# One decoder step on Trainium2: three slabs for the modulation weights, SSM-table stores on another queue, a bias broadcast in four later pieces, state copies after the attention

## The chip, the cores and the metric

The kernel runs on one core of a Trainium2 chip. The metric is the device time of one execution in microseconds (us). Engines are called as in the profile: PE (TensorE, PEld its weight loads), DVE (VectorE), ACT (ScalarE), POOL (GpSimd), SP (SyncE, which here does nothing but issue transfers). A "q" behind an engine's name is its sequencer, the part that waits on semaphores and issues transfers.

## What is computed

One layer of a hybrid decoder for a prompt of 1024 tokens and 8 sample rows, all in float32. The part that matters here, cut from the reference:

```
def adaln(c, w, b):
    m = (jax.nn.silu(c) @ w + b)[:, None, :]          # 9 rows x 6144 columns
    return jnp.split(m, 6, axis=-1)
def shared_bias(table, dist):
    bt = table[rel_bucket(dist)]                       # 8 heads
    return jnp.moveaxis(bt, -1, 0).reshape(N_KV_HEADS, GQA, *dist.shape)
```

Around it stand a state-space model (SSM, "S5") on half of the mixer's channels, attention with that bias on the other half (compressed, selected and window keys), and a top-4-of-32 mixture of experts. One of the outputs, win_kv_sample, is the sample rows' window state of 512 tokens moved on by one token.

## The kernel before

The program is one stream of stages; a scheduler turns the order in which the instructions are written into a fixed order on each engine.

1. **Before the mixer, 0 to 403 us.** Five jobs are written in turns, as the string ORDER (line 35) says: `adaln` (24 turns "r"), `compress_sample` (the sample rows' cache), the statistics of x, `ssm_prep` (turn "S") and `bias_prep` (turn "B"). Then `mixer_x` normalizes x.
   - `adaln` loads w_ada in 24 slabs `wt` of 128x8x256 (1 MB each, on SP, L499) into two buffers; each slab feeds 8 matmuls (L504), and the next load into a buffer waits for these.
   - `compress_sample` transposes gathered cache rows `rr` on PE (L1155), splits them into `xh` (ACT, L1157) and `xl` (DVE, L1158) and multiplies them (L475 to L477).
   - `ssm_prep` computes, in 8 iterations over groups g0, the tables of the SSM: six products on POOL (`lmul`, L885), transposes on PE into `o1` (L922), a product with `v1` (L937), copies on ACT (L924 to L926, L938), sums on DVE. Each iteration stores `o1` (L927), `v1` (L933), `wt` (L947) to `ssmw` and zeros (`zt`, L940) and `kt` (L941) to `ssmk`, all on SP. The name `tp` is a PSUM buffer, `wt` here another tile than adaln's.
   - `bias_prep` stores a row of 1152 biases for each of 8 heads (`bt`, L1249) and copies each 128 times, from DRAM to DRAM, to `bx` (L1251, 4.7 MB), which the attention reads back (`tt`, L1305) with a skewed pattern.
2. **Mixer, 403 to 685 us** (`mixer`, L633). Seven blocks of 256 columns, a = 0, 256, ..., 1536. In each, for the 8 row tiles t, 24 matmuls (L475 to L477) fill a PSUM bank. For a < 512 ACT copies it to a tile `kv` (L689; two buffers) and SP stores it to `ud` (L690). From a = 256 to a < 1280 one of the 16 steps of `ssm` is written at each odd t: a step loads `w` (L976) and `m` (L980) of the tables and `hs` (L1023, L1024), every fourth step also `ur` from `ud` (L970), then transposes (`up`, L986) and goes through DVE and ACT; at its end it stores `hb` (L1052).
3. **Attention, 685 to 1200 us.** It reads `bx`, stores its result (`attd`, L1389, on SP); the sample rows' part copies 511 rows of window state from DRAM to DRAM for each of 8 sample rows (L1700, 0.5 MB each, on SP). The scheduler has put these copies into stage 1.
4. **Mixture of experts, 1200 to 3207 us**: weight streams and matmuls with an order of their own.

On each queue the transfers are issued in order. A transfer counts on one of eight semaphores of its queue, taken in turn.

Of the kernel before, what the change touches and what calls it, by code (L numbers as in the profile page):

```python
# [10 lines left out]
F = mybir.dt.float32  # L11
# [11 lines left out]
D = 1024  # L23
B = 8
NT = T // 128
KT = D // 128
# [424 lines left out]
class K:  # L451
# [28 lines left out]
    def adaln(self, c):  # L480
        nc, tc, i = self.nc, self.tc, self.i
        self.md = tc.dram_tile([9, 6144], F, name="md")
        p = self.pool("ada", ctx=c)
        w = self.pool("adaw", bufs=2, ctx=c)
        q = self.pool("adaq", bufs=1, psum=True, ctx=c)
        cs, sg = (w.tile([128, KT, 256], F, name="wt").rearrange("p k f -> p (k f)")[:9, :D] for _ in range(2))
        nc.sync.dma_start(out=cs[0:8], in_=i["c_sample"])
# [8 lines left out]
        for n in range(24):  # L496
            s = slice(n * 256, (n + 1) * 256)
            wt = w.tile([128, KT, 256], F, name="wt")
            nc.sync.dma_start(out=wt, in_=i["w_ada"][0].rearrange("(k p) f -> p k f", p=128)[:, :, s])  # L499
            bt = w.tile([9, 256], F, name="bt")  # L500
            nc.scalar.dma_start(out=bt, in_=i["b_ada"][:, s].to_broadcast([9, 256]))
            po = q.tile([128, 256], F, name="po")[:9]
            for k in range(KT):
                last = nc.tensor.matmul(po, lhsT=ct[:, k], rhs=wt[:, k], start=k == 0, stop=k == KT - 1)  # L504
            self.ada.append(last.ins)
            mt = w.tile([9, 256], F, name="mt")
            one = 1.0 if n // 4 in (1, 4) else 0.0
            nc.vector.scalar_tensor_tensor(out=mt, in0=po, scalar=one, in1=bt, op0=ALU.add, op1=ALU.add)
            nc.scalar.dma_start(out=self.md[:, s], in_=mt)
            yield  # L510
# [53 lines left out]
    def mixer_x(self):  # L564
        nc, i = self.nc, self.i
        p, q, hp, mv, rs = self.csp, self.csq, self.hp, self.mv, self.rs
# [3 lines left out]
        rows = p.tile([16, 128], F, name="fold", bufs=2)  # L570
# [5 lines left out]
        for t in range(NT):  # L576
# [16 lines left out]
            (nc.vector if t in ON_DVE2 else nc.gpsimd).tensor_tensor(out=self.hl[:, :, s], in0=h32, in1=self.hh[:, :, s].bitcast(F), op=ALU.subtract)  # L593
        xq, sh, sc = (p.tile([8, D], F, name="rr", bufs=4) for _ in range(3))
        nc.sync.dma_start(out=xq, in_=i["x_sample"][:, 0])
# [37 lines left out]
    def mixer(self, ctx):  # L633
# [9 lines left out]
        with ExitStack() as c:  # L643
# [4 lines left out]
            for m, (a, n) in enumerate(((0, 256), (256, 256), (512, 256), (768, 256), (1024, 256), (1280, 256), (1536, 280))):  # L648
# [31 lines left out]
                for t in range(NT):  # L680
# [6 lines left out]
                    if a < 512:  # L687
                        ut = p2.tile([128, 256], F, name="kv")
                        nc.scalar.activation(out=ut, in_=po[:, :256], func=AF.Copy)  # L689
                        nc.sync.dma_start(out=self.ud.rearrange("m t f -> (m t) f")[rows, a:a + 256], in_=ut)  # L690
                    elif a < 1024:
# [77 lines left out]
    def ssm_prep(self):  # L769
# [11 lines left out]
        with ExitStack() as c:  # L781
# [128 lines left out]
            zt = p.tile([16, 4, 128], F, name="zt")  # L910
            g_.memset(zt, 0.0)
            p2 = self.pool("sp2", bufs=2, ctx=c)
            for g0 in range(0, 32, 4):
# [12 lines left out]
                nc.scalar.activation(out=o1[:, 1, :, 64:128], in_=tp[:, :, 0:64], func=AF.Copy, scale=-1.0)  # L926
                nc.sync.dma_start(out=self.wd_[:, 0:2, gs], in_=o1)  # L927
                v1 = p2.tile([128, 4, 9, 16], F, name="v1")
# [3 lines left out]
                v.tensor_tensor(out=v1, in0=v1, in1=w2, op=ALU.add)  # L932
                nc.sync.dma_start(out=self.wd_[:, 2, gs], in_=v1[:, :, 1:9].rearrange("p g k c -> p g (k c)"))  # L933
                kt = p2.tile([16, 4, 8, 16], F, name="kt")
# [4 lines left out]
                v.tensor_tensor(out=kt[:, :, 0], in0=kt[:, :, 0], in1=dd[:, gs], op=ALU.add)  # L939
                nc.sync.dma_start(out=self.kd[:, gs, 0:8].rearrange("c g k d -> c g (k d)"), in_=zt)  # L940
                nc.sync.dma_start(out=self.kd[:, gs, 8:16].rearrange("c g k d -> c g (k d)"), in_=kt.rearrange("c g k d -> c g (k d)"))  # L941
                wt = p2.tile([128, 4, 8, 16], F, name="wt")
# [3 lines left out]
                v.tensor_tensor(out=wt, in0=wt, in1=w2[:, :, 0:8], op=ALU.subtract)  # L946
                nc.sync.dma_start(out=self.wd_[:, 3, gs], in_=wt.rearrange("p g k c -> p g (k c)"))  # L947

# [169 lines left out]
    def compress_sample(self):  # L1118
# [16 lines left out]
        for b in range(B):  # L1135
            rr = []
# [6 lines left out]
            for ch in range(4):  # L1143
                after = self.ada[-1:][:1] if 4 * b + ch >= 8 else []
                with self.tc.issue_after(after[0]) if after else ExitStack():
# [3 lines left out]
                    for s in range(2):  # L1149
                        r = p.tile([128, 16, 64], F, name="rr", bufs=4)  # L1150
                        nc.vector.tensor_copy(out=r, in_=rr[s][:, ch])
# [63 lines left out]
    def bias_prep(self):  # L1215
# [6 lines left out]
        with ExitStack() as c:  # L1222
# [26 lines left out]
            nc.sync.dma_start(out=self.bt, in_=bv)  # L1249

            nc.sync.dma_start(out=self.bx, in_=self.bt[:, None].to_broadcast([8, 128, 1152]))  # L1251

# [25 lines left out]
    def attention(self):  # L1278
# [3 lines left out]
        with ExitStack() as c:  # L1282
# [78 lines left out]
            def values(g, t, pr):  # L1361
# [26 lines left out]
                v.tensor_tensor(out=at[hi], in0=ov[hi, :, 1], in1=sh[hi], op=ALU.add)  # L1388
                nc.sync.dma_start(out=self.att[:, 2 * g:2 * g + 2, rows], in_=at)  # L1389

# [212 lines left out]
    def sample_attention(self, bank):  # L1603
# [75 lines left out]
        with ExitStack() as c:  # L1679
# [14 lines left out]
            for b in range(B):  # L1694
# [4 lines left out]
                flat = [d[0, b].rearrange("t c h d -> (t c h d)") for d in (self.o["win_s"], i["state_win_kv"])]  # L1699
                nc.sync.dma_start(out=flat[0][0:511 * 256].rearrange("(a f) -> a f", a=128), in_=flat[1][256:512 * 256].rearrange("(a f) -> a f", a=128))  # L1700
                tp = bank(128, 4, 128)
# [618 lines left out]
```

## Time and profile before

| | |
|---|---|
| runs shown | median 3202.93 us of 3 (3199.05 to 3207.68) |
| profiled execution | 3209.21 us, span 3207.4 us, mean granted clock 0.946 |
| busy share of the span | PE 93%, DVE 72%, ACT 56%, POOL 11% |
| stage 1, 0 to 403 us | PE busy 313.1 us (68.34, 63.46, 162.52 and 18.80 in four stretches) |
| mixer, 403 to 685 us | PE busy 280.4 us |
| attention and on, 685 to 1200 us | PE busy 473.5 us |
| experts, 1200 to 3207 us | PE busy 1905.0 us |

A row of a table by stretches gives the stretch and its length, the busy time of PE, PEld, DVE, ACT and POOL with their instructions, the granted clock of PE (1.00 is the full 2.4 GHz, 0.50 is 1.2 GHz), the busy share of the core's 16 DMA engines, and GB/s. A row of a list of waits gives the waiting engine and line, what it waited for, the sum in us, how often, and the longest. In a timeline a row is start, duration, engine, line, operation, and in brackets the idle time before it and what ended it.

### The profile page before, as it was taken

To read this page: it belongs to the slowest core of one execution; us is meant where nothing else is said; L and a number is where in the kernel's file an instruction comes from. 1 tells how busy PE (TensorE), PEld (TensorE's weight loads), DVE (VectorE), ACT (ScalarE), POOL (GpSimd) and SP (SyncE) were. 2 spreads that over 40 slices of the span, in tenths; PEclk is the share of its full clock that TensorE was granted. 3 is DMA by queue.
4 is the path that set the end of the run, shared out by engine and by line. 5 is a ranking of instruction groups with operands and counts; after the bars stand their busy time and mean duration, and the time that the engine had idled before them with its cause. 6 is when DMAs were issued, how large, how long until landed. Compare 5 with 4: busy or idle time off the path is not lost. (4 is left out here: it accounts for less than half of the span.)

```text
span 3207.4 us, 51067 instructions
## 1 busy us (share of the span) xinstructions
PE 2972.0 (93%) x15681; PEld 2380.6 (74%) x15682; DVE 2321.0 (72%) x4434; ACT 1785.9 (56%) x2824; POOL 358.7 (11%) x467
## 2 busy tenths in 40 slices
PE   7787899998999898599999999999999999999977
PEld 4555699976778586378887887888887888878752
DVE  5654846448777688688878868775689865796978
ACT  3332635456657643377667656564477654675751
POOL 1620121002311000100000000000000000000013
PEclk9888899988879799699999999999999999999988
DMA  8766343223512342798979869764289915792926
GB/s 287 250 219 226 126 124 106 85 74 83 132 29 65 126 152 80 264 335 288 315 228 369 277 230 360 233 238 139 77 281 371 337 68 190 242 368 100 350 84 275
DMA packets 445575, 656.33 MB, mean 205 GB/s; under 512 B 45455, under 2 KB 371072, under 8 KB 441265
## 3 DMA queue, kind: packets, MB, share of 16 engines
q1 hardware_dynamic: 418290, 535.40, 49.7%
q0 software_dynamic: 24464, 115.59, 10.4%
q10 hardware_dynamic: 2704, 3.85, 0.3%
q8 instruction: 64, 1.05, 0.1%
q14 instruction: 53, 0.43, 0.0%
HBM read 594.95 MB, written 68.73 MB: 207 GB/s over the span
## 5 line engine op out<-in xcount | busy, mean ns | idle before, releaser
L272 DVE TENSOR_TENSOR lo<-raw,hi 128x1024 fp32r<-128x1024 f32 x870 | 1030.9, 1221 | 307.3 <-ACT hi L199 302.3
L199 ACT ACTIVATE hi<-raw 128x1024 fp32r<-128x1024 f32 x870 | 916.3, 1060 | 491.9 <-PE pc L388 490.7
L386 PE MATMUL pc<-hi,X 128*128 128x512 f32 x1408 | 561.0, 398 | 4.7 <-DVE X L277 3.8
L388 PE MATMUL pc<-hi,X 128*128 128x512 f32 x1408 | 550.8, 391 | 0.0
L387 PE MATMUL pc<-lo,X 128*128 128x512 f32 x1408 | 549.8, 390 | 0.0
L386 PEld LDWEIGHTS pc<-hi,X 128*128 128x128 f32 x1408 | 265.2, 188 | 60.6 <-issue 8.9
L388 PEld LDWEIGHTS pc<-hi,X 128*128 128x128 f32 x1408 | 264.9, 188 | 56.6
L387 PEld LDWEIGHTS pc<-lo,X 128*128 128x128 f32 x1408 | 265.5, 189 | 51.5
L386 PE MATMUL pc<-hi,HT 128*128 128x512 f32 x704 | 282.6, 401 | 12.1 <-DVE HT L294 9.0
L388 PE MATMUL pc<-hi,HT 128*128 128x512 f32 x704 | 274.8, 390 | 0.0
L387 PE MATMUL pc<-lo,HT 128*128 128x512 f32 x704 | 274.6, 390 | 0.0
L386 PEld LDWEIGHTS pc<-hi,HT 128*128 128x128 f32 x704 | 132.2, 188 | 53.4 <-issue 28.5
L388 PEld LDWEIGHTS pc<-hi,HT 128*128 128x128 f32 x704 | 132.2, 188 | 28.3
L1319 DVE CUSTOM_DVE_ANT_0 pt<-sc,tt 128x512 f32<-128x512 f32 (+7 forms) x256 | 107.3, 436 | 61.5 <-PE sc L1335 29.1
L387 PEld LDWEIGHTS pc<-lo,HT 128*128 128x128 f32 x704 | 132.4, 188 | 24.9
L475 PE MATMUL po<-wih,hh 128*128 128x256 f32 (+3 forms) x504 | 147.6, 293 | 0.0
L476 PE MATMUL po<-wil,hh 128*128 128x256 f32 (+3 forms) x504 | 146.9, 292 | 0.0
L477 PE MATMUL po<-wih,hl 128*128 128x256 f32 (+3 forms) x504 | 145.8, 289 | 0.0
L504 PE MATMUL po<-wt,ct 128*9 128x256 f32 x384 | 102.6, 408 | 38.6 <-DMA wt<-in_w_ada_dram 36.9
L421 POOL DMA_INDIRECT xg<-hd,ic x52 | 65.4, 1257 | 589.2 <-PE px L354 558.2
L1157 ACT ACTIVATE xh<-tp 128x512 fp32r<-128x512 f32 x128 | 71.3, 594 | 89.1 <-PE tp L1155 80.6
L1372 PE MATMUL tp<-ident,pt 128*128 128x128 f32 (+6 forms) x592 | 115.3, 306 | 4.4 <-DVE pt L1358 4.0
(698 smaller groups left out, 5742.6 us busy)
## 6 DMA issues: line engine op xcount, KB each, us to landing
raw<-in_w_gate_up_dram SPq DMA_DIRECT2D x248, 1024.0 KB, 10.0
raw<-in_w_down_dram SPq DMA_DIRECT2D x64, 2048.0 KB
wt<-in_w_ada_dram SPq DMA_DIRECT2D x24, 1024.0 KB
yd<-yt SPq DMA_DIRECT2D x44, 512.0 KB
w<-ssmw SPq DMA_DIRECT2D x16, 512.0 KB
raw<-in_w_gate_up_dram POOLq DMA_DIRECT2D x8, 1024.0 KB
wir<-in_w_in_dram SPq DMA_DIRECT2D x20, 256.0 KB
bx<-bt SPq DMA_DIRECT2D x1, 4608.0 KB
```

Of the source, the lines that this page charges most:

```text
L199: A.activation(out=hi[:,u%H],in_=rawview(u),func=AF.Copy).then_inc(S['hi'][u],1)
L272: V.tensor_tensor(out=lo[:,u%H],in0=rawview(u),in1=hi[:,u%H].bitcast(F),op=ALU.subtract).then_inc(S['lo'][u],1)
L386: PE.matmul(o,lhsT=sH,rhs=wh,start=kt==0,stop=False)
L387: PE.matmul(o,lhsT=sH,rhs=wl,start=False,stop=False)
L388: ins=PE.matmul(o,lhsT=sL,rhs=wh,start=False,stop=kt==7)
L475: pe.matmul(o, lhsT=lh, rhs=rh, start=start, stop=False)
L476: pe.matmul(o, lhsT=lh, rhs=rl, start=False, stop=False)
L477: return pe.matmul(o, lhsT=ll, rhs=rh, start=False, stop=stop)
L504: last = nc.tensor.matmul(po, lhsT=ct[:, k], rhs=wt[:, k], start=k == 0, stop=k == KT - 1)
L1157: nc.scalar.activation(out=xo, in_=tp, func=AF.Copy)
L1319: v.tensor_tensor_reduce(out=pt[:, off[r] + a:off[r] + a + n], in0=sc, in1=bias, scale=1.0, scalar=-3e38, op0=ALU.add, op1=ALU.max, accum_ ...
L1372: pe.transpose(tp[:n, h * 128:h * 128 + 128], pr[h][:, a:a + n], self.ident)
```

## The change

- `adaln`: three buffers for the slabs `wt` in place of two; the buffers `rr` of `compress_sample` and `mixer_x` go from four to three.
- `ssm_prep`: all stores are issued on ACT; the eight stores of zeros stand ahead of the 8 iterations.
- `bx`: the one broadcast of L1251 becomes four of two heads each (1.18 MB), on SP, each right behind the store to `ud` of t = 1, 3, 5, 7 in the mixer's block a = 256.
- the 8 copies of the window state are held behind the last attention store written before them.

```
-        cs, sg = (w.tile([128, KT, 256], F, name="wt")...
+        cs, sg = (w.tile([128, KT, 256], F, name="wt", bufs=3)...
...
-            wt = w.tile([128, KT, 256], F, name="wt")
+            wt = w.tile([128, KT, 256], F, name="wt", bufs=3)
...
-                        r = p.tile([128, 16, 64], F, name="rr", bufs=4)
+                        r = p.tile([128, 16, 64], F, name="rr", bufs=3)
...
-                        nc.sync.dma_start(out=self.ud...[rows, a:a + 256], in_=ut)
+                        st = nc.sync.dma_start(out=self.ud...[rows, a:a + 256], in_=ut)
+                        if a == 256 and t % 2:
+                            hs = slice(t - 1, t + 1)
+                            with self.tc.issue_after(st.ins):
+                                nc.sync.dma_start(out=self.bx[hs], in_=self.bt[hs, None].to_broadcast([2, 128, 1152]))
...
+            for g0 in range(0, 32, 4):
+                nc.scalar.dma_start(out=self.kd[:, g0:g0 + 4, 0:8]..., in_=zt)
...
-                nc.sync.dma_start(out=self.wd_[:, 0:2, gs], in_=o1)
+                nc.scalar.dma_start(out=self.wd_[:, 0:2, gs], in_=o1)
...
-                nc.sync.dma_start(out=self.kd[:, gs, 0:8]..., in_=zt)
...
-            nc.sync.dma_start(out=self.bx, in_=self.bt[:, None].to_broadcast([8, 128, 1152]))
...
-                nc.sync.dma_start(out=self.att[:, 2 * g:2 * g + 2, rows], in_=at)
+                self.put = nc.sync.dma_start(out=self.att[:, 2 * g:2 * g + 2, rows], in_=at).ins
...
-                nc.sync.dma_start(out=flat[0]..., in_=flat[1]...)
+                with self.tc.issue_after(self.put):
+                    nc.sync.dma_start(out=flat[0]..., in_=flat[1]...)
```

The stores of `v1`, `kt` and `wt` change in the same way as that of `o1`. In the changed kernel L922 is L929, L937 is L944, L924 to L926 are L931 to L933, the stores L927, L933, L941, L947 are L934, L940, L947, L953, L976 is L982, L980 is L986, L986 is L992, L1155 is L1161; the pieces of `bx` are L695.

The scheduler gives the engines another order. Three places follow.

**PE, the last iterations of `ssm_prep`.** Before, the transposes L922 and the products L937 of an iteration stand among slabs of `adaln` (L504) and transposes of `compress_sample` (L1155):

```order
L922 MATMUL tp<-ident,wt 128x128 x4
L937 MATMUL tp<-v_1110,bst 16x128 x4
L504 MATMUL po<-wt,ct 9x256 x8
L1155 MATMUL tp<-ident,rr 128x128 x7
L922 MATMUL tp<-ident,wt 128x128 x4
L1155 MATMUL tp<-ident,rr 128x128
L937 MATMUL tp<-v_1147,bst 16x128 x4
L1155 MATMUL tp<-ident,rr 128x128 x8
L504 MATMUL po<-wt,ct 9x256 x3
L922 MATMUL tp<-ident,wt 128x128 x4
```

After the change:

```order
L1161 MATMUL tp<-ident,rr 128x128 x7
L929 MATMUL tp<-ident,wt 128x128 x4
L944 MATMUL tp<-v_1151,bst 16x128 x4
L929 MATMUL tp<-ident,wt 128x128 x4
L944 MATMUL tp<-v_1187,bst 16x128 x4
L929 MATMUL tp<-ident,wt 128x128 x4
L944 MATMUL tp<-v_1223,bst 16x128 x4
L929 MATMUL tp<-ident,wt 128x128 x4
L944 MATMUL tp<-v_1259,bst 16x128 x4
L1161 MATMUL tp<-ident,rr 128x128 x4
```

The last four iterations follow each other with nothing between. Between the first transpose L922 and the last product L937 of all eight, the order before has 133 matmuls of L475 to L477, 84 transposes L1155 and 30 matmuls L504; the order after has 24, 22 and 16. The rest stands ahead: 72, 42 and 15 more than before precede the first transpose.

**ACT, two iterations of `ssm_prep` after the change.** Before, ACT held only the four copies here, among those of `compress_sample`, and the stores stood on SP between the loads L499:

```order
L931 ACTIVATE o_1110<-tp 128x512
L932 ACTIVATE o_1110<-tp 128x4x64
L933 ACTIVATE o_1110<-tp 128x4x64
L940 DMA ssmw<-v_1115 128x4x128
L934 DMA ssmw<-o_1110 128x2x512
L945 ACTIVATE kt<-tp 16x512
L953 DMA ssmw<-wt 128x512
L947 DMA ssmk<-kt 16x4x128
L931 ACTIVATE o_1146<-tp 128x512
```

The four stores of an iteration now stand between its copies and those of the next one.

**SP, the block a = 256 of the mixer.** After the change (the stores to `ud` here are those of t = 1 to 5; before, the same kinds of rows stand here without the broadcasts, with the loads of `w` and `m` further ahead):

```order
L690 DMA ud<-kv 128x256
L695 DMA bx<-bt 256x1x1152
L690 DMA ud<-kv 128x256
L1058 DMA out_dram<-hb 8x2x64 x2
L690 DMA ud<-kv 128x256
L695 DMA bx<-bt 256x1x1152
L690 DMA ud<-kv 128x256
L986 DMA m<-ssmk 128x1x128
L1029 DMA hs<-in_state_ssm_re_dram 8x2x64
L1030 DMA hs<-in_state_ssm_im_dram 8x2x64
L690 DMA ud<-kv 128x256
L695 DMA bx<-bt 256x1x1152
```

The stores to `ud` and a load of `m` are queued behind pieces of the broadcast. On PE, the second half of that step now stands behind 49 projection matmuls, and the whole block a = 512 (8 times 24 matmuls) stands before the products of step 3; between the end of step 3 and the `up` transposes of step 4 (L992) there is none of these, where the order before has 53.

## Rows read from the trace of the kernel before

**Rows 1.** Busy time of each engine over the span, from the page.

```profile
PE 2972.0 (93%) x15681; PEld 2380.6 (74%) x15682; DVE 2321.0 (72%) x4434; ACT 1785.9 (56%) x2824; POOL 358.7 (11%) x467
```

**Rows 2.** Table by stretches, the time before the mixer.

```profile
0.00:93.00 93.00, 68.34 (x406) 49.05 (x407) 57.34 (x168) 31.58 (x54) 15.49 (x24) 0.98 0.84 274
93.00:178.00 85.00, 63.46 (x374) 43.74 (x374) 57.46 (x75) 29.20 (x62) 58.69 (x49) 0.84 0.66 236
178.00:373.00 195.00, 162.52 (x1055) 113.96 (x1054) 109.20 (x215) 68.10 (x129) 10.87 (x19) 0.91 0.59 217
```

**Rows 3.** Waits of PE, 0 to 403 us.

```profile
PE po L504 <- DMA wt<-in_w_ada_dram: 36.9, 4, 16.5
```

**Rows 4.** Waits of SP's queue, 0 to 403 us.

```profile
SPq L499 <- PE po L504: 112.7, 16, 14.2
SPq L927 <- ACT o L926: 38.0, 6, 13.0
```

**Rows 5.** Timeline of PE at these waits, and of SP ahead of the longest.

```profile
144.18 2.30 PE L504 MATMUL po<-wt,ct 128*9 128x256 f32 x5 [7.03 <-DMA wt<-in_w_ada_dram]
...
198.90 5.58 PE L504 MATMUL po<-wt,ct 128*9 128x256 f32 x16 [9.55 <-DMA wt<-in_w_ada_dram]
204.41 0.77 PE L1155 MATMUL tp<-ident,rr 128*128 128x128 f32 x5
...
257.93 0.77 SPq L1251 DMA_DIRECT2D bx<-bt  x1
265.73 24.87 SPq L499 DMA_DIRECT2D wt<-in_w_ada_dram  x2
...
280.22 0.28 PE L476 MATMUL po<-xl,w1h 128*128 128x256 f32 x1
280.34 0.28 PE L477 MATMUL po<-xh,w1l 128*128 128x256 f32 x1
297.07 2.30 PE L504 MATMUL po<-wt,ct 128*9 128x256 f32 x5 [16.45 <-DMA wt<-in_w_ada_dram]
```

**Rows 6.** Table by stretches, while the broadcast moves, and around the wait.

```profile
261.00:270.00 9.00, 8.81 (x56) 5.77 (x56) 4.75 (x9) 3.24 (x8) 0.10 (x1) 1.00 0.51 209
...
290.00:297.00 7.00, 0.00 (x0) 0.00 (x0) 0.00 (x0) 0.00 (x0) 0.00 (x0) 0.50 0.89 307
297.00:322.00 25.00, 24.21 (x137) 14.55 (x138) 9.55 (x17) 6.48 (x13) 0.10 (x1) 0.90 0.36 123
```

**Rows 7.** Timeline of POOL, the same product of three iterations in a row.

```profile
88.07 1.06 POOL L885 TENSOR_TENSOR wt<-pw,bst 128x512 f32<-128x512 f32 x1
...
96.75 1.50 POOL L885 TENSOR_TENSOR wt<-pw,bst 128x512 f32<-128x512 f32 x1
...
106.61 1.06 POOL L885 TENSOR_TENSOR wt<-pw,bst 128x512 f32<-128x512 f32 x1
```

**Rows 8.** Groups of PE, the slabs' matmuls over the span, from the page.

```profile
L504 PE MATMUL po<-wt,ct 128*9 128x256 f32 x384 | 102.6, 408 | 38.6 <-DMA wt<-in_w_ada_dram 36.9
```

**Rows 9.** Table by stretches, the mixer's blocks with SSM steps, and the attention.

```profile
436.00:548.00 112.00, 112.00 (x1016) 106.15 (x1015) 65.68 (x223) 55.70 (x125) 18.02 (x50) 1.00 0.39 115
...
685.00:1200.00 515.00, 473.46 (x2717) 377.08 (x2718) 379.03 (x1391) 318.87 (x751) 66.17 (x87) 0.86 0.33 96
```

**Rows 10.** Timeline of SP, block a = 256 of the mixer.

```profile
445.05 0.36 SPq L690 DMA_DIRECT2D ud<-kv  x1
...
447.01 0.34 SPq L690 DMA_DIRECT2D ud<-kv  x1
...
457.07 0.35 SPq L690 DMA_DIRECT2D ud<-kv  x1
```

**Rows 11.** Transposes `up` (L986), two a step: ns, first and last start.

```profile
L986 PE MATMUL up<-ident,ug x32: 271/272/273, 436.0 to 603.3; 128*128 128x128 f32 x32
```

**Rows 12.** The copies to `kv` (L689): what ACT waited for before them.

```profile
  DMA ud<-kv: 2.7, 1
```

**Rows 13.** The copies of the window state, from the list of transfers.

```profile
out_dram<-in_state_win_kv_dram SPq DMA_DIRECT2D x8, 511.0 KB
```

More of the change, by code (lines that the diff above doesn't have):

```diff
@@ L485, in adaln @@
         q = self.pool("adaq", bufs=1, psum=True, ctx=c)
-        cs, sg = (w.tile([128, KT, 256], F, name="wt").rearrange("p k f -> p (k f)")[:9, :D] for _ in range(2))
+        cs, sg = (w.tile([128, KT, 256], F, name="wt", bufs=3).rearrange("p k f -> p (k f)")[:9, :D] for _ in range(2))
         nc.sync.dma_start(out=cs[0:8], in_=i["c_sample"])
@@ L593, in mixer_x @@
             (nc.vector if t in ON_DVE2 else nc.gpsimd).tensor_tensor(out=self.hl[:, :, s], in0=h32, in1=self.hh[:, :, s].bitcast(F), op=ALU.subtract)
-        xq, sh, sc = (p.tile([8, D], F, name="rr", bufs=4) for _ in range(3))
+        xq, sh, sc = (p.tile([8, D], F, name="rr", bufs=3) for _ in range(3))
         nc.sync.dma_start(out=xq, in_=i["x_sample"][:, 0])
@@ L689, in mixer @@
                         nc.scalar.activation(out=ut, in_=po[:, :256], func=AF.Copy)
-                        nc.sync.dma_start(out=self.ud.rearrange("m t f -> (m t) f")[rows, a:a + 256], in_=ut)
+                        st = nc.sync.dma_start(out=self.ud.rearrange("m t f -> (m t) f")[rows, a:a + 256], in_=ut)
+                        if a == 256 and t % 2:
+                            hs = slice(t - 1, t + 1)
+                            with self.tc.issue_after(st.ins):
+                                nc.sync.dma_start(out=self.bx[hs], in_=self.bt[hs, None].to_broadcast([2, 128, 1152]))
                     elif a < 1024:
@@ L911, in ssm_prep @@
             g_.memset(zt, 0.0)
+            for g0 in range(0, 32, 4):
+                nc.scalar.dma_start(out=self.kd[:, g0:g0 + 4, 0:8].rearrange("c g k d -> c g (k d)"), in_=zt)
             p2 = self.pool("sp2", bufs=2, ctx=c)
@@ L932, in ssm_prep @@
                 v.tensor_tensor(out=v1, in0=v1, in1=w2, op=ALU.add)
-                nc.sync.dma_start(out=self.wd_[:, 2, gs], in_=v1[:, :, 1:9].rearrange("p g k c -> p g (k c)"))
+                nc.scalar.dma_start(out=self.wd_[:, 2, gs], in_=v1[:, :, 1:9].rearrange("p g k c -> p g (k c)"))
                 kt = p2.tile([16, 4, 8, 16], F, name="kt")
@@ L939, in ssm_prep @@
                 v.tensor_tensor(out=kt[:, :, 0], in0=kt[:, :, 0], in1=dd[:, gs], op=ALU.add)
-                nc.sync.dma_start(out=self.kd[:, gs, 0:8].rearrange("c g k d -> c g (k d)"), in_=zt)
-                nc.sync.dma_start(out=self.kd[:, gs, 8:16].rearrange("c g k d -> c g (k d)"), in_=kt.rearrange("c g k d -> c g (k d)"))
+                nc.scalar.dma_start(out=self.kd[:, gs, 8:16].rearrange("c g k d -> c g (k d)"), in_=kt.rearrange("c g k d -> c g (k d)"))
                 wt = p2.tile([128, 4, 8, 16], F, name="wt")
@@ L946, in ssm_prep @@
                 v.tensor_tensor(out=wt, in0=wt, in1=w2[:, :, 0:8], op=ALU.subtract)
-                nc.sync.dma_start(out=self.wd_[:, 3, gs], in_=wt.rearrange("p g k c -> p g (k c)"))
+                nc.scalar.dma_start(out=self.wd_[:, 3, gs], in_=wt.rearrange("p g k c -> p g (k c)"))
     def ssm(self, c):
@@ L1699, in sample_attention @@
                 flat = [d[0, b].rearrange("t c h d -> (t c h d)") for d in (self.o["win_s"], i["state_win_kv"])]
-                nc.sync.dma_start(out=flat[0][0:511 * 256].rearrange("(a f) -> a f", a=128), in_=flat[1][256:512 * 256].rearrange("(a f) -> a f", a=128))
+                with self.tc.issue_after(self.put):
+                    nc.sync.dma_start(out=flat[0][0:511 * 256].rearrange("(a f) -> a f", a=128), in_=flat[1][256:512 * 256].rearrange("(a f) -> a f", a=128))
                 tp = bank(128, 4, 128)
```

## The prediction

> **What bounds the kernel now.** I read the page first: PE is busy 93% of the span [rows 1], so a change counts by the PE idle time that it removes or adds, or by PE's clock. The table by stretches shows where idle time is left ahead of the mixer: 93.0 - 68.3 = 24.7 us, 85.0 - 63.5 = 21.5 us and 195.0 - 162.5 = 32.5 us in three stretches, 78.7 us together [rows 2]. The list of PE's waits there names the largest: 36.9 us in four waits for slabs of `adaln` [rows 3]. They are 7.03, 9.55 and 16.45 us in the timeline [rows 5], and the fourth is what is left, 3.9 us, in the first stretch. The list for SP's queue tells why slabs are late: a slab waits for its buffer (112.7 us), and SP stands still behind SSM stores whose data are not ready, 38.0 us for those of `o1` alone [rows 4]. The longest PE wait has another neighbour: after the broadcast of `bx` at 257.93, the next two slab issues take SP 24.87 us, and PE gets its slab at 297.07 [rows 5]. In the mixer's SSM blocks there is nothing to win: PE is busy 112.0 of 112.0 us at granted clock 1.00 [rows 9]. Any stall put there is paid in full. In the attention PE has 515.0 - 473.5 = 41.5 us of idle time and the DMA engines a share of 0.33 [rows 9].
>
> **The change ahead of the mixer.** The third slab buffer, the stores taken off SP, the broadcast and the state copies taken out of the stage all work at those four waits. I let them go: -3.9 us in the first stretch, -7.0 in the second, -9.6 and -16.5 (26.0 together) in the third. What is late next is `ssm_prep`. Its eight iterations now stand close together on PE, and each needs six products on POOL. POOL is busy 58.7 us in the second stretch [rows 2], 58.7 / 8 = 7.3 us an iteration if nothing holds it; the starts of one product lie 8.7 and 9.9 us apart [rows 7]. In the order after, POOL's gathers mostly stand elsewhere, but each iteration also waits on ACT, where four stores stand between its copies and the next one's (an issue on SP is 0.35 us [rows 10]). I take 8.1 us, between the two, 65 us for eight.
>
> PE's work in those 65 us: the 63.5 us of the second stretch, less what moved out. A matmul of `compress_sample` starts 0.12 us after the one before it and a transpose takes 0.77 / 5 = 0.15 us [rows 5]; a matmul of a slab is 102.6 / 192 = 0.53 us (the 384 records are two for each of 24 x 8) [rows 8]. Moved out are 133 - 24 = 109, 84 - 22 = 62 and 30 - 16 = 14 of these: 13.1 + 9.3 + 7.4 = 29.8 us. So 33.7 us stay, and PE idles 65 - 34 = 31 us there, where it idled 21.5. The idle time ahead of the mixer becomes 20.8 + 31 + 6.5 = 58.3 in place of 78.7, -20.4 us. Behind the longest wait the granted clock was 0.50 and then 0.90 on average over 25 us [rows 6]; without it these 25 us give back some 2. **This term: -22 us.** Bounds: at 7.3 us an iteration the idle time there is 25, so -29, and with some of the other waits of the stage -35. At 9.3 us (the mean of the two distances) it is 41, so -12, and if half of the 26 us stays as waits for slabs, +1. `rr` with three buffers in place of four costs nothing while slabs or POOL set the pace; without that cover it is within these bounds.
>
> **The broadcast in the mixer.** The old transfer has eight heads in its outermost dimension; while it moves, the DMA share is 0.51, about 8 of 16 engines, at 209 GB/s [rows 6], so one engine seems to carry one head: 4.72 MB / 209 GB/s = 22.6 us. A piece has two heads. Its bytes on each of two engines are those of the old transfer, so a piece lasts 22.6 us too, four one behind the other 90 us. A store to `ud` or a load of `m` uses all engines, and its shares on the two busy ones are queued behind the piece. The trace shows no such piece, so the ends are: each on engines of its own (all four overlap), or all on the same two. I take the same two, because the one transfer that is shown had a fixed set and nothing in the second differs but its address; this decides most of the forecast.
>
> The Trainium skill, "DMA: Bandwidth & Descriptors", section "Why a DMA increments its semaphore by 16 and not by 1", says that the engines used are the largest number up to 16 that divides the outermost dimension on both sides, and the lowest-numbered ones. The trace agrees on the number (0.51 for eight heads [rows 6]); which engines, no run here shows yet. By it the pieces share two engines and the sum is the one below; by the other end it is about 40 us less.
>
> On the clock of before: the store of t = 1 is issued at 445.05 [rows 10], piece 1 right behind it and done at 468. The store of t = 2 (447.01) lands then. `kv` has two buffers, so the copy of t = 4, which came just ahead of the store at 457.07 [rows 10], waits until 468. That this wait exists the rows on that copy show, 2.7 us once [rows 12]. PE goes on with t = 5 and then lacks a bank, about 464 to 468: **5 us**. The store of t = 4 goes out at 469 behind piece 2, which ends at 491. The copy of t = 6 waits for it, and so does a load of `m` that step 2 needs. PE has t = 6 and t = 7 left, some 49 matmuls of 0.12 us, until about 474: **18 us** of idle time. Step 2 ends with little beside it: **4 us**. Then the block a = 512, 8 x 24 matmuls and its transposes, covers piece 3 (to 514). Step 3 stands alone on PE behind it. A step came every 167.3 / 15 = 11.2 us [rows 11], of which 48 projection matmuls took 48 x 0.12 = 5.8, so without them some 6 us of its chain show; and step 4's loads are queued behind piece 4, until 537, which I price at as much again: **12 us**. Steps 4 to 9 stand close together with 85 projection matmuls where there were 48 to a step, with DVE ahead of PE: **5 us**. **This term: +44 us.** Bounds: overlapping pieces end by 469 and 492, and by that the second stall is about 3 us and the third and fourth mostly gone, +10; if every us of the four pieces were paid, +90.
>
> **The rest.** The state copies move 8 x 0.5 MB [rows 13] in a stage whose DMA share is 0.33 [rows 9]; at 300 GB/s (the rate at share 0.89 is 307 [rows 6]) that is 14 us of all engines over some 500. I take +1, for loads that stand behind them, between -3 and +6. The experts' 2007 us are not touched.
>
> **Sum.** -22 + 44 + 1 = +23 us on the profiled execution's 3209 us, 3232. That execution is 6.3 us over the median of the runs shown, 3202.9; on that basis the time is **3226 us**.
>
> **The rivals.**
> A. **The pieces cost little, faster.** If the four transfers overlap, or their shares spread over many engines, the mixer loses 10 us or less and the sum is -22 + 10 + 1 = -11, **3192 us**; with nothing lost 3182. For: PE had the copies' wait only once before [rows 12], and the DMA share in the block is 0.39 [rows 9]. Against: a share of 0.51 for eight heads [rows 6], which says few engines for few heads. The mechanism decides at the store of t = 4: if it lands before 474 in the clock above, the kernel is faster. The point is a loss of 12 us in the mixer.
> B. **They cancel.** A gain of 33 us ahead of the mixer (7.3 us an iteration, clock kept) and a loss of 33 (the copies' stalls, but steps 3 to 9 hidden): **3203 us**. For: POOL's pace of 7.3 [rows 2]. Against: ACT's queue now has the stores.
> C. **The bunched iterations eat the gain.** With 9.3 us an iteration and slabs still late, the first term is about 0: +45, **3248 us**. For: distances of 8.7 and 9.9 us [rows 7].
> D. **The waits for slabs stay.** If the slabs are late because of the DMA engines (share 0.84 in the first stretch [rows 2]) and not of buffers and SP's queue, the change does not do what it says; a part of C's price.
>
> **How the numbers follow.** About 0.3%, 9.6 us, is what a measurement of this kernel can tell from no change. The forecast, which spans 3210 to 3242 by its own bounds, 0.47; A 0.22; B 0.19; C and D 0.12. Faster takes A and little else: 0.22; the same (3193 to 3213) B and the low edge of the forecast: 0.21; slower 0.57. The range leaves out A's lowest tenth and all four pieces in full: 3188 to 3258.
>
> **What would show it.** Ahead of the mixer: the four waits L504 gone but for a few us, the mixer's first matmul some 22 us earlier, PE idle some 30 us between the first L929 and the last L944. In the mixer: copies to `kv` that wait for `ud`, stretches with the DMA share near 2/16 = 0.13, and PE idle some 40 us between 410 and 530. If the share there is far above 0.13 or PE stays busy, the second term is wrong, and A holds; if waits for slabs stay above 15 us, the first.

## The result, and the profile after

The change makes the kernel slower: 3289.1 us, median of 4 runs (3280.3 to 3292.6), against 3204.3 us of the kernel before in the same runs; the ratio is 1.0256, 95% interval 1.0233 to 1.0279. The forecast was 3226 with a range up to 3258: the sign was right, the loss is 85 us in place of 23.

Both profiles can be cut at the same events: the first matmul behind the loads of phi_w (L1092, now L1098), the first transpose of `mixer_x` (L584), the first load of `tt`, the last attention store, the experts' first gather (L421). The cuts are starts read from the timelines.

| us | before | after | difference | forecast |
|---|---|---|---|---|
| start to first matmul | 13.1 | 26.1 | +13.0 | 0 |
| first matmul to `mixer_x` | 360.1 | 355.5 | -4.6 | -22 |
| `mixer_x` and mixer | 310.8 | 366.0 | +55.2 | +44 |
| attention | 412.1 | 417.6 | +5.5 | +1 |
| to the experts' first gather | 227.6 | 227.1 | -0.5 | 0 |
| experts | 1883.7 | 1895.2 | +11.5 | 0 |
| span | 3207.4 | 3287.4 | +80.0 | +23 |

The lists of PE's waits of the changed kernel, ahead of the mixer (to 382 us), and then in it (382 to 748):

```profile
PE po L1098 <- DMA fold<-in_phi_pe_dram: 21.9, 1, 21.9
PE tp L929 <- DVE wt L926: 18.5, 5, 6.4
PE po L476 <- DVE xl L1164: 14.8, 3, 12.8
PE tp L1161 <- DVE xl L1164: 14.8, 4, 7.3
```

```profile
PE po L475 <- ACT kv L689: 24.5, 2, 14.4
PE up L992 <- DVE ug L989: 9.6, 1, 9.6
```

The 36.9 us of waits for slabs [rows 3] are gone altogether; there is no such row any more. In their place PE waits for `ssm_prep`'s sums (L926) and for `xl`, which DVE computes among and behind the work of `ssm_prep`, and, ahead of all, 21.9 us for the loads of phi. The table by stretches (start to the first L929, the eight iterations, the rest to `mixer_x`), whose counterparts are [rows 2]:

```profile
0.00:132.00 132.00, 92.00 (x552) 66.06 (x554) 69.54 (x192) 40.64 (x72) 17.47 (x27) 0.96 0.69 232
132.00:207.00 75.00, 35.15 (x175) 21.61 (x173) 38.90 (x40) 15.06 (x34) 55.40 (x46) 0.71 0.58 199
207.00:382.00 175.00, 165.35 (x1114) 120.96 (x1114) 116.74 (x227) 73.98 (x141) 10.49 (x18) 0.97 0.55 191
```

The eight iterations take 75 us, of which PE works 35.2: it idles 40 us where 31 were forecast, at granted clock 0.71. From the first matmul to `mixer_x`, outside the iterations and with the waits for slabs left aside, it idles 23.9 us in place of 15.0, with 16.9 us of waits for `xl` in place of 4.9.

In the mixer the stalls stand where they were forecast. The timeline of SP, and then that of ACT:

```profile
454.24 0.67 SPq L695 DMA_DIRECT2D bx<-bt  x1
455.79 9.28 SPq L690 DMA_DIRECT2D ud<-kv  x1
...
468.43 0.85 SPq L695 DMA_DIRECT2D bx<-bt  x1
```

```profile
480.78 0.38 ACT L689 ACTIVATE kv<-po 128x256 f32<-128x256 f32 x1 [9.13 <-DMA ud<-kv]
...
503.91 0.38 ACT L689 ACTIVATE kv<-po 128x256 f32<-128x256 f32 x1 [12.30 <-DMA ud<-kv]
```

The store of t = 2 is issued behind the first piece; the copy of t = 4, which waits for it, starts at 480.78, 26 us behind the piece, and the copy of t = 6 at 503.91, another 23 us later. The table by stretches, from where PE has run dry behind the first piece:

```profile
470.00:480.00 10.00, 0.93 (x6) 0.69 (x6) 1.53 (x5) 1.20 (x3) 0.61 (x1) 0.69 0.13 53
...
490.00:515.00 25.00, 10.65 (x74) 8.43 (x75) 2.83 (x10) 3.92 (x10) 0.62 (x2) 0.66 0.17 65
515.00:535.00 20.00, 19.86 (x161) 18.68 (x161) 3.47 (x5) 7.09 (x12) 0.00 (x0) 1.00 0.24 85
535.00:560.00 25.00, 15.62 (x123) 13.50 (x121) 6.71 (x19) 6.81 (x14) 1.89 (x5) 0.78 0.19 66
560.00:600.00 40.00, 35.93 (x286) 31.96 (x287) 27.33 (x108) 18.03 (x43) 8.40 (x24) 0.84 0.49 144
```

A DMA share of 0.13 is two engines of sixteen, and 53 GB/s is about a quarter of the 209 GB/s of eight [rows 6]. The granted clock, 1.00 in this block before [rows 9], is 0.66 to 0.69 around the stalls up to 515 us, and again 0.78 and 0.84 from 535 to 600. The rows from `mixer_x` to `tt`, of the kernel before and then of the changed one:

```profile
373.20:684.00 310.80, 298.76 (x2515) 278.13 (x2516) 155.54 (x477) 146.32 (x344) 51.21 (x104) 0.96 0.33 95
```

```profile
382.00:748.00 366.00, 315.21 (x2515) 288.73 (x2513) 154.60 (x481) 141.32 (x339) 52.31 (x105) 0.89 0.31 94
```

PE's idle time grows by 38.8 us (12.0 to 50.8). Its busy time grows by 16 us for the same 2515 matmul records: by the clock records of the trace, work at granted clock 0.50 loses 22 us there in place of 9, some 14 of the 16.

### The profile page after: what moved, and what is told of

Its sections match the earlier page's. It is cut to its first block, busy times and chain, and to the rows that moved or that the text cites. A ratio compares the mean times of both kernels' runs of the same rounds, so it can differ in the third digit from the quotient of the medians.

```text
span 3287.4 us, 51080 instructions
## 1 busy us (share of the span) xinstructions
PE 2987.0 (91%) x15681; PEld 2390.9 (73%) x15682; DVE 2325.3 (71%) x4434; ACT 1781.3 (54%) x2820; POOL 359.4 (11%) x467
## 5 line engine op out<-in xcount | busy, mean ns | idle before, releaser
L386 PE MATMUL pc<-hi,X 128*128 128x512 f32 x1408 | 560.8, 398 | 4.7 <-DVE X L277 3.8
L386 PEld LDWEIGHTS pc<-hi,X 128*128 128x128 f32 x1408 | 265.0, 188 | 61.2 <-issue 8.8
L386 PE MATMUL pc<-hi,HT 128*128 128x512 f32 x704 | 282.6, 401 | 22.4 <-DVE ut L293 11.5
L386 PEld LDWEIGHTS pc<-hi,HT 128*128 128x128 f32 x704 | 132.2, 188 | 65.0 <-issue 40.1
L475 PE MATMUL po<-wih,hh 128*128 128x256 f32 (+3 forms) x504 | 149.2, 296 | 24.5 <-ACT kv L689 24.5
L477 PE MATMUL po<-wih,hl 128*128 128x256 f32 (+3 forms) x504 | 147.1, 292 | 0.0
L421 POOL DMA_INDIRECT xg<-hd,ic x52 | 61.6, 1185 | 591.0 <-PE px L354 560.2
L1353 ACT ACTIVATE pt<-pt,mx 128x640 f32<-128x640 f32 (+15 forms) x192 | 112.2, 589 | 9.2 <-DVE mx L1350 9.1
L1379 ACT ACTIVATE th<-tp 128x512 fp32r<-128x512 f32 (+5 forms) x148 | 83.0, 590 | 61.6 <-PE tp L1376 54.7
```

Of the source, the lines that this page charges most:

```text
L386: PE.matmul(o,lhsT=sH,rhs=wh,start=kt==0,stop=False)
L475: pe.matmul(o, lhsT=lh, rhs=rh, start=start, stop=False)
L477: return pe.matmul(o, lhsT=ll, rhs=rh, start=False, stop=stop)
L1353: A.activation(out=o, in_=o, func=AF.Exp, bias=mx[:, h, r:r + 1], accum_out=sm[:, h, r:r + 1])
L1379: A.activation(out=th[:n], in_=tp[:n], func=AF.Copy)
```

## The experiments

The cuts of every run's profile, in us, and its median against the kernel before on the same chip. Differences of a few us between single profiles of the attention are not read: the first four kernels, whose attention is the same, give 397 to 421.

| run | first matmul | to `mixer_x` | mixer | attention | experts | median, ratio (95%) |
|---|---|---|---|---|---|---|
| the change | 26.1 | 355.5 | 366.0 | 417.6 | 1895.2 | 3289.1, 1.0256 (1.0233 to 1.0279) |
| wide_pieces | 15.4 | 358.1 | 312.7 | 397.3 | 1895.5 | 3232.8, 1.0081 (1.0051 to 1.0110) |
| whole_broadcast | 25.8 | 361.0 | 311.0 | 411.4 | 1894.7 | 3232.3, 1.0072 (1.0048 to 1.0096) |
| zeros_later | 24.0 | 353.9 | 366.7 | 420.8 | 1896.2 | 3284.1, 1.0238 (1.0211 to 1.0266) |
| three_slabs_alone | 24.5 | 338.8 | 312.3 | 403.6 | 1894.7 | 3201.3, 0.9972 (0.9952 to 0.9991) |
| before_again | 26.9 | 358.7 | 310.8 | 406.5 | 1882.3 | 3214.9, one run |
| stores_on_sp | 14.5 | 335.3 | 311.8 | 406.8 | 1895.3 | 3209.5, 0.9992 (0.9973 to 1.0010) |
| pieces_alone | 25.5 | 338.9 | 367.3 | 403.0 | 1883.5 | 3240.5, 1.0087 (1.0061 to 1.0113) |
| slabs_wide_broadcast | 24.2 | 331.5 | 311.7 | 416.5 | 1897.1 | 3199.6, 0.9947 (0.9927 to 0.9968) |
| o1_on_act | 25.4 | 338.8 | 310.9 | 415.8 | 1896.3 | 3215.4, 1.0025 (1.0005 to 1.0045) |
| before_8_more_dve | 24.8 | 358.1 | 310.9 | 411.9 | 1895.6 | 3217.6, 1.0024 (1.0005 to 1.0042) |
| slabs_wide_27_dve | 25.8 | 336.2 | 311.4 | 408.1 | 1896.4 | 3200.5, 0.9964 (0.9947 to 0.9982) |
| slabs_wide_123_dve | 14.0 | 342.9 | 311.0 | 411.8 | 1895.5 | 3202.6, 0.9978 (0.9956 to 0.9999) |
| slabs_wide_3_less_dve | 24.8 | 332.4 | 311.0 | 404.6 | 1881.9 | 3184.3, 0.9919 (0.9891 to 0.9947) |
| slabs_wide_gathers_held | 15.4 | 335.3 | 311.2 | 397.4 | 1883.4 | 3181.8, 0.9920 (0.9898 to 0.9941) |

### The pieces of the broadcast

**wide_pieces** keeps the four places and turns each piece round.

```
-  nc.sync.dma_start(out=self.bx[hs], in_=self.bt[hs, None].to_broadcast([2, 128, 1152]))
+  nc.sync.dma_start(out=self.bx[hs].rearrange("h r f -> r h f"), in_=self.bt[None, hs].to_broadcast([128, 2, 1152]))
```

> The change, with the four pieces of the broadcast at the same places but with the 128 copies as the outermost dimension of both sides in place of the two heads. Theory (few engines): a piece then spreads over 16 engines, lasts about 4 us in place of 23, no store to ud is held up, and the time from mixer_x's first transpose (L584) to the first load of tt falls from 366 us to about 311, as before the change: total about 3234. Rival (the place in the block costs, whatever the engines: traffic of 1.2 MB beside the SSM loads): the mixer stays above 340 us, total above 3260.

The mixer is back at 312.7 us; the median is 3232.8 (the profiled run, 3208.8, is the fastest of five). Its timeline of SP, and then its table by stretches, behind the first piece:

```profile
445.81 0.64 SPq L695 DMA_DIRECT2D bx<-bt  x1
447.35 0.35 SPq L690 DMA_DIRECT2D ud<-kv  x1
454.58 0.35 SPq L690 DMA_DIRECT2D ud<-kv  x1
```

```profile
450.00:453.00 3.00, 3.00 (x32) 2.79 (x31) 2.33 (x7) 1.27 (x4) 0.61 (x2) 1.00 0.83 317
```

The stores to `ud` leave at the old distances of 2 and 7 us (before: 445.05 and 447.01 [rows 10], then 454.23), the piece moves at a share of 0.83, and PE is busy all the time. The bytes and the places are the same, so it is not 4.7 MB beside the SSM loads that cost. What costs is the two engines, with the order that goes with them: the scheduler also gave this kernel the old order of the SSM steps, so the run does not separate the stalls from the bunched steps. The waits above put 24.5 us on `kv` alone.

**pieces_alone** has nothing but the four narrow pieces of the change on the kernel before.

```
-            nc.sync.dma_start(out=self.bx, in_=self.bt[:, None].to_broadcast([8, 128, 1152]))
...
+                            with self.tc.issue_after(st.ins):
+                                nc.sync.dma_start(out=self.bx[hs], in_=self.bt[hs, None].to_broadcast([2, 128, 1152]))
```

> The kernel before with the broadcast in the four pieces of the change and nothing else: stage 1 has the order of before, the mixer that of the change. Theory (two engines carry all four pieces, and PE runs dry behind them): from mixer_x to the first load of tt about 365 us in place of 311, +55 us, less up to 16 us for the slabs' wait that goes with the broadcast out of stage 1: total 3245 to 3265. Rival (the mixer's loss needs the change's stage 1): below 330 us, total below 3220.

Mixer 367.3 us, +56.5; from the first matmul to `mixer_x` 338.9, -20 to -21 against the two profiles of before; median +28 us, 4.5 us under the range expected. So the mixer's loss needs nothing of the change's stage 1. The waits for slabs fall from 36 to 18.9 us, so taking the broadcast out of stage 1 is worth 20 us there, and the place that it was put costs almost three times that.

**whole_broadcast** puts it back into `bias_prep` and leaves the rest of the change.

```
+            nc.sync.dma_start(out=self.bx, in_=self.bt[:, None].to_broadcast([8, 128, 1152]))
...
-                            with self.tc.issue_after(st.ins):
-                                nc.sync.dma_start(out=self.bx[hs], ...
```

> The change, with the broadcast whole and back in bias_prep; three slabs, stores on ACT and late state copies stay. Theory: the mixer is back at about 311 us as in the run with wide pieces, and the third slab covers the broadcast ahead of the mixer, so the total is within 5 us of that run, about 3234 to 3240. Rival (the broadcast beside the slabs was what made the old 16.5 us wait): that wait comes back, and the total is 10 to 16 us above the run with wide pieces.

The mixer is at 311.0, there is no wait for a slab, and the median is that of wide_pieces: the third slab covers the broadcast, as the theory had it. But both runs stay 22 us above the kernel before. The experts' 12 us are in that (below); what the third slab gives, something else of the change takes back.

### Stage 1: slabs and stores

**three_slabs_alone**: the third slab (and three `rr`) on the kernel before.

```
-            wt = w.tile([128, KT, 256], F, name="wt")
+            wt = w.tile([128, KT, 256], F, name="wt", bufs=3)
```

> The kernel before, with three slabs for w_ada and three buffers for rr, and nothing else of the change. Theory (the slabs' waits come from buffers and SP's queue): the four waits for slabs, 36.9 us, shrink to under 15, and the mixer begins 10 to 25 us earlier: total 3180 to 3195. Rival (what the third slab gives is taken by the SSM iterations and by rr): the mixer begins within 5 us of 373, total 3200 to 3210.

The waits for slabs fall from 36.9 to 4.8 us and the stage by some 20 us (338.8 against 360.1 and 358.7). The median, 3201.3, lies above the range expected (3180 to 3195), only 9.6 us below the kernel before: the experts take back 12 (below).

**stores_on_sp** differs from whole_broadcast in the queue of the SSM stores alone.

```
-                nc.scalar.dma_start(out=self.wd_[:, 0:2, gs], in_=o1)
+                nc.sync.dma_start(out=self.wd_[:, 0:2, gs], in_=o1)
```

(and the same for `v1`, `kt`, `wt` and the zeros)

> Three slabs and late state copies, with the broadcast whole in bias_prep and the SSM stores back on SP, zeros among them. Against the run with the whole broadcast, only the queue of the stores differs. Theory (on ACT's queue the stores hold the copies of the next iteration and let the scheduler put the eight iterations close together, with PE idle between): from the first L922 to mixer_x about 232 us, as with three slabs alone, in place of 255, total about 20 us less, 3212. Rival (the queue of the stores does not matter; the late state copies or the broadcast cost the 23 us): from the first L922 to mixer_x still 250 or more.

From the first matmul to `mixer_x` 335.3 us in place of 361.0, median 22.7 us less. The lists of waits around the eight iterations, of whole_broadcast, ACT from 132 to 207 us and then PE from 120 to 215:

```profile
ACT o L926 <- DVE kt L941: 19.5, 2, 10.9
ACT o L926 <- DMA ssmw<-o: 12.5, 2, 8.8
ACT o L926 <- DVE mt L508: 10.7, 1, 10.7
```

```profile
PE tp L924 <- DVE wt L921: 17.6, 5, 6.4
PE tp L1156 <- DVE xl L1159: 13.1, 2, 7.4
PE po L476 <- DVE xl L1159: 12.7, 1, 12.7
```

then of stores_on_sp, PE in the same window:

```profile
PE tp L922 <- DVE wt L919: 5.3, 3, 2.7
PE tp L922 <- DVE kt L939: 3.9, 2, 3.4
PE po L476 <- DVE xl L1158: 2.4, 2, 2.1
```

and the two kernels' tables by stretches for the iterations, whole_broadcast first:

```profile
132.00:206.00 74.00, 35.06 (x178) 21.90 (x176) 38.85 (x40) 15.21 (x35) 55.59 (x46) 0.71 0.59 202
```

```profile
122.00:191.00 69.00, 53.87 (x310) 35.68 (x309) 49.52 (x62) 23.73 (x53) 55.13 (x47) 0.88 0.70 235
```

POOL is busy 55 us in both. With the stores on SP the iterations take 5 us less, and PE works 19 us more in them: it idles 15.1 us there in place of 38.9, which is nearly all of the 26. With the stores on ACT, ACT stands 19.5 us at the store of `kt` until DVE has finished it, and the copies behind it come late. The same wait in the changed kernel's timeline of ACT and its queue (L947 is the store of `kt`, L931 the next iteration's first copy):

```profile
163.99 0.34 ACTq L953 DMA_DIRECT2D ssmw<-wt  x1
171.85 0.33 ACTq L947 DMA_DIRECT2D ssmk<-kt  x1
172.28 0.60 ACT L931 ACTIVATE o<-tp 128x512 f32<-128x512 f32 x1 [10.80 <-DVE kt L946]
```

**o1_on_act** leaves `v1`, `kt`, `wt` and the zeros on SP and puts only `o1`, ACT's own result, on ACT.

```
-                nc.sync.dma_start(out=self.wd_[:, 0:2, gs], in_=o1)
+                nc.scalar.dma_start(out=self.wd_[:, 0:2, gs], in_=o1)
```

> The run with the stores on SP, with the stores of o1 alone moved to ACT, which computes o1; v1, wt and kt, which DVE finishes, and the zeros stay on SP. Theory (on ACT the stores cost by what they wait for, the sums of DVE behind POOL's products; a store of ACT's own result waits for nothing): from the first matmul after the loads of phi_w to mixer_x 332 to 342 us, as with all stores on SP (335), total within 5 us of it, about 3205 to 3214. Rival (any store in ACT's queue lengthens the iterations): 348 us or more, total above 3220.

338.8 us, 3.5 above all stores on SP, and the median is at 3215.4, 6 above and just over the range expected. So of the 26 us some 22 come from the stores that wait for DVE and the zeros, and a few from `o1`. What of the 22 is ACT standing at a store, and what the order that the scheduler makes because of it (24 matmuls of L475 to L477 among the iterations in place of 96), these runs do not separate. PE's idle time in the iterations goes with that order: 39 us with 24 such matmuls among them, 22 with 81 (o1_on_act), 15 with 96, and 18 with 98 (three_slabs_alone, whose iterations take 75 us too).

**The state copies.** stores_on_sp and three_slabs_alone differ in them alone: late in the first, early in the second. The two have 335.3 and 338.8 us to `mixer_x`, 406.8 and 403.6 us in the attention, medians 2.5 and 9.6 us below before, and their intervals overlap: the pair alone decides nothing. All medians together speak against the late copies. From each median's distance to the kernel before, take what the kernel's profile adds to `mixer_x`, in the mixer and in the experts (against the means of the two profiles of before, 359.4, 310.8 and 1883.0). Of the six kernels with late copies five are left with 8 to 12 us and the change with 21; the eight with early ones are left with -8 to +2. So the late copies seem to cost some 10 us. Where, the single profiles do not show, since their attention differs by over 20 us for other reasons.

### The late start

**zeros_later** holds the eight stores of zeros back.

```
-            for g0 in range(0, 32, 4):
-                nc.scalar.dma_start(out=self.kd[:, g0:g0 + 4, 0:8]..., in_=zt)
...
+                with self.tc.issue_after(neg.ins):
+                    nc.scalar.dma_start(out=self.kd[:, gs, 0:8]..., in_=zt)
```

(`neg` is the third of the copies to `o1`)

> The change, with the eight stores of zeros each held behind the o1 copies of its own iteration, still on ACT, in place of the first microseconds. Theory (the zeros, issued at 1.9 to 6.3 us ahead of the loads of phi_w, push these into the gathers of the cache): PE's first wait falls from 21.9 to about 9 us, w1h is computed at about 11 us in place of 26, and the total falls by 10 to 13 us, to about 3277. Rival (the start is late for another reason, the gathers or SP's longer issues): first wait stays above 18 us and the total does not move.

My theory fell: the first matmul is at 24.0 us all the same, and the median is within the spread of the change. **before_again** shows that the change has no part in it.

> The kernel before, once more, for a second profile of it. Theory (the late start is a matter of chance: whether the loads of phi_w land before the gathers of the cache fill the DMA engines): the first matmul behind them may begin at 13 us or at 24 to 26 us here too, and the experts' part, 1884 us in the first profile and 1895 in all others so far, is about 1895. Rival (the change made the start late and the experts slower): 13 us and 1884 again.

The kernel before has the late start too. Its waits of PE from 0 to 385 us:

```profile
PE po L504 <- DMA wt<-in_w_ada_dram: 36.0, 4, 16.7
PE po L1092 <- DMA fold<-in_phi_pe_dram: 22.6, 1, 22.6
```

So the 13 us of the first row of the table above are chance between two profiles, not the change; the first profile had the early start, one of four among the 15 profiles that hold no gather back (wide_pieces, with its zeros ahead on ACT, is another). The other half of the theory missed: the experts take 1882.3 us here, as in the first profile, so their 12 us are no chance.

### The experts

**before_8_more_dve**, **slabs_wide_27_dve**, **slabs_wide_123_dve** and **slabs_wide_3_less_dve** move DVE's code. The first adds to the kernel before

```
+        pad = p.tile([1, 1], F, name="pad")
+        for _ in range(8):
+            nc.vector.memset(pad, 0.0)
```

and the two after it add 27 and 123 such memsets to **slabs_wide_broadcast**, which is three_slabs_alone with the broadcast turned round as a whole:

```
-            nc.sync.dma_start(out=self.bx, in_=self.bt[:, None].to_broadcast([8, 128, 1152]))
+            nc.sync.dma_start(out=self.bx.rearrange("h r f -> r h f"), in_=self.bt[None].to_broadcast([128, 8, 1152]))
```

> The kernel before with three slabs, and the whole broadcast in bias_prep with its 128 copies as the outermost dimension. Theory: the broadcast takes about 12 us of all engines in place of 23 us of eight, the slabs' waits all but go, mixer_x begins by 363 us or earlier, and the total is that of three slabs alone or up to 5 us less: 3190 to 3201, 10 to 15 us below the kernel before on the same chip. Rival (all 16 engines taken at once hold up the slabs more than eight did): a slab's wait of over 8 us comes back, total above 3205.

The waits for slabs are 0.5 us and the stage is 331.5 us, 7 less than with the slabs alone; the median, 12.4 us below before, is in the expected range.

> The kernel before with eight one-element memsets more on DVE at the start of adaln, so that all of DVE's later code lies eight instructions further on. Theory (the experts' 12 us that every kernel with three slabs lost go with the place of DVE's code, 3397 and 3400 instructions without, 3402 to 3421 with the loss): the experts' part takes 1895 us in place of 1883. Rival (they go with the third slab itself): 1883.

1895.6 us. Eight memsets at the start, and no third slab, cost the experts 12 us. What DVE waited for ahead of L293 (an operation on `ut` that reads what the one before it wrote), of the kernel before, and then with the eight memsets:

```profile
  DVE ut L293: 25.4, 84
```

```profile
  DVE ut L293: 33.9, 84
  DVE ut L292: 2.6, 16
```

and PE's waits for it (L386), of the change, then with the eight memsets, then of slabs_wide_3_less_dve, whose row is also that of the kernel before:

```profile
PE pc L386 <- DVE ut L293: 11.5, 21, 0.7
```

```profile
PE pc L386 <- DVE ut L293: 11.2, 21, 0.7
```

```profile
PE pc L386 <- DVE ut L293: 1.9, 4, 0.5
```

The experts' instructions and their durations (L293: medians of 406 and of 425 to 427 ns in all) are the same; the pause between two dependent DVE instructions is 25.4 / 84 = 0.30 us or 33.9 / 84 = 0.40 us. PE's longer waits behind them, 11.2 in place of 1.9 us, are some 9 of the 12 us.

> Three slabs and the wide whole broadcast, with 27 one-element memsets more on DVE: 3429 instructions, 32 more than the kernel before has. Theory (place of code, repeating every 32 instructions): the experts' part is back at 1883 us and the total 10 to 12 us below the run without them. Rival (third slab, or a longer period): 1895.

> The same with 123 memsets: 3526 instructions, 129 more than the kernel before, so next to its place for any period of 32, 64 or 128. Theory (place of code): the experts' part at 1883 us, the total 5 to 12 us below the run without memsets, since 123 memsets take some 7 us of DVE at the start, most of them while it waits for loads. Rival (third slab): 1895.

Both stay long, at 1896.4 and 1895.5 us: the place of the code does not repeat every 32, 64 or 128 instructions, as these two were to find out.

> Three slabs and the wide whole broadcast, with three memsets (half_pi, qk, qp) moved from DVE to POOL: 3399 DVE instructions, between the two counts that had the short experts' part (3397 and 3400). Theory (place of DVE's code alone): the experts' part at 1883 us, the total 10 to 13 us below the run with 3402, about 3188, and 20 or more below the kernel before. Rival (something else of the three slabs and of the memsets adds up to the same 12 us): 1895, total 3200.

```
-        v.memset(self.qk, 0.0)
+        nc.gpsimd.memset(self.qk, 0.0)
```

(and the same for `half_pi` and `qp`) 1881.9 us with three slabs, and the median is 25.6 us below the kernel before on its chip, where it was 12.4 us without. Counts of 3397, 3399 and 3400 DVE instructions in the program have the short experts' part; 3402, 3405 and 3414 to 3526 the long one. So the time goes with how many instructions DVE's program has ahead of the experts, and with it the place of their code. Why, and whether it is the place as such, the profiles do not show.

**slabs_wide_gathers_held** adds to slabs_wide_3_less_dve a copy on POOL that reads the loads of phi_w ahead of the second gather.

```
+        self.seen = nc.gpsimd.tensor_copy(out=p.tile([128, 2, 8, 2, 1], F, name="seen"), in_=w1[:, :, :, :, 0:1])
...
+                with self.tc.issue_after(self.seen.ins) if t in (1, 2) else ExitStack():
                     nc.gpsimd.indirect_dma_start(out=raw, ...
```

> The same, with the second and third gather of the cache held on POOL until the loads of phi_w have landed (a copy of 32 elements on POOL that reads them). Theory (the late start is the loads of phi_w caught behind 6 MB of gathers): PE's first matmul behind these loads begins at 12 to 15 us in every run, the spread of the runs falls from some 25 us to under 15, and the median is 5 to 10 us below the run without the hold. Rival (loads behind one gather are caught too, or the gathers now come late): first matmul at 18 us or more, or the first transposes of rr wait instead, no gain in the median.

The one profile starts at 15.4 us, and the runs lie within 18.6 us (3172.7 to 3191.3) where they lay within 30 without the hold. The median is 2.5 us lower, which is less than the spread tells: inconclusive as to the time, and one profile does not show that the start is now always early. Both last kernels beat the kernel before by 0.8% (ratios 0.9919 and 0.9920).

## Why the prediction was wrong

The sign, the end of the waits for slabs and the places of the stalls in the mixer were right. The size was not, and neither was what the stores cost on ACT. Of the 57 us between +23 and the profiles' +80:

1. **The pieces' term, +44, measured +55.2** (56.5 in pieces_alone). The choice that decided it, all four pieces on the same two engines, holds: a share of 0.13 while one moves, and copies released 23 us apart. The Trainium skill ("DMA: Bandwidth & Descriptors", "Why a DMA increments its semaphore by 16 and not by 1") says that a transfer issued on SP takes the lowest-numbered of the engines; the trace agrees that the pieces share their two, with those 23 us, and does not show which two they are. The step that failed is in the pricing of the stalls: 44 us of idle time were summed (38.8 measured), and PE's clock was left at 1.00. It was 0.66 to 0.84 in most of the time from 470 to 600 us, which is some 14 of the other 16 us.
2. **The first term, -22, measured -4.6** from the first matmul on. "I let them go" was right for the four waits for slabs (36.9 to 0). What failed is "I take 8.1 us, between the two" and, with it, that the stores on ACT cost little more than their issue: the iterations came every 75 / 8 = 9.4 us, just past the upper bound of 9.3, and PE idled 40 us there in place of 31. Outside them, where the forecast only took the slabs' waits away, PE idled 9 us more, mostly for `xl`. Rival C had this pace, with 12% together with D, though it took slabs to be late as well. stores_on_sp prices the stores on ACT: 26 us. With the stores left on SP, the third slab is worth 20 to 25 us (338.8 and 335.3 us in place of 360.1 and 358.7), about what I had forecast for the whole; third slab and moved broadcast together, without the stores on ACT, were not run.
3. **"The experts' 2007 us are not touched" was wrong by 11.5 us.** No instruction of theirs was edited; what lies ahead of them on DVE changed. Eight idle memsets do the same.
4. **13 us are the first profile's luck.** The sum was made against a profile with an early start, which the kernel before has in some executions only. The step "that execution is 6.3 us over the median" did not see that its parts lay on both sides. This share belongs to the profiles and is not in the medians.
5. **The state copies' +1, between -3 and +6, was probably too little.** The profile has 5.5 us more attention, in a spread of over 20 us; the medians of all kernels put the late copies at some 10 us.

The medians are 85 us apart. Stage, mixer and experts give 64 of these and the state copies some 10; the other 10 stay open. zeros_later, which differs from the change in the zeros alone, loses 73 us and leaves nothing open.

Rival A failed at the point that was named for it. The store of t = 4 landed when the copy of t = 6 could start, at 503.9; piece 1 was issued at 454.2 in place of 445.4, so that is 495 on the clock of before, not 474. Rival B would have needed ACT's stores to cost nothing. Rival D fell with the waits for slabs.

## What to carry to other kernels

Put the dimension of 128 outermost in a broadcast between DRAM buffers. The Trainium skill ("DMA: Bandwidth & Descriptors", "Rules for kernel authors") asks for an outermost dimension that is a multiple of 16; here the mixer lost 55 us to four transfers with two heads outermost, and 2 us when the same bytes had the 128 copies outermost. A store belongs on a queue whose engine has nothing else to do until its data are ready; on ACT, stores that waited for DVE's sums cost as much as the third slab had won. When a change moves the time in a part of the program that it doesn't touch, take a second profile of the kernel before and add a few idle instructions to it, before looking for a cause in the change.

## What was not expected

The number of DVE instructions in the program goes with 12 us of the experts' 1883: 84 pauses between dependent DVE instructions last 0.30 or 0.40 us, and PE's waits behind them are 1.9 or about 11 us; eight instructions more switch it, three fewer switch it back. The first matmul behind the loads of phi_w begins at 13 to 15 us or at 24 to 27; it may be that these loads, 1 MB, land before or behind 6 MB of gathers, but the one run that holds gathers back does not settle it. And the issue of a store to `ud` on SP, 0.35 us in this block before [rows 10], took up to 9.28 us behind a narrow piece, so that queue itself stood still, not only the transfers in it.
